# Weight sums loaded three rounds ahead in more buffers, and the sample attention stepped once in two places of a tile

## The chip, the cores and the metric

The kernel runs on one NeuronCore of a Trainium2 chip. The metric is the device time of one execution in microseconds (us). TensorE (PE) multiplies, VectorE (DVE), ScalarE (ACT) and GpSimd (POOL) do the elementwise work, and SyncE (SP) issues nearly all transfers. Each engine runs its own instructions strictly in order; what one engine needs of another, or of a transfer, is a semaphore wait ahead of the instruction.

## The reference

One layer of a hybrid decoder over a prompt of 2064 tokens (16 learned ones in front) and 8 samples of 4 tokens each:

```python
q, k, v, u = in_project(hp, norm_mix_pre[l], w_in[l])
att_o = swa_prompt(q, k, v, attn_sinks[l])           # sliding window of 128
ssm_o, hr, hi = ssm_mixer(u, ...)                     # complex diagonal scan, half-GLU
hp = hp + merge_out(att_o, ssm_o, ..., w_out[l], norm_mix_post[l])
hp = hp + sqrelu_mlp(hp, norm_mlp_pre[l], w_up[l], w_down[l], norm_mlp_post[l])
...                                                   # the same for the samples hs, with
att_o, nk, nv = swa_sample(q, k, v, cache_k_win[l], cache_v_win[l], pos_s, attn_sinks[l])

def sqrelu_mlp(h, g_pre, w_up, w_down, g_post):
    hn = rmsnorm(h, g_pre)
    a = jnp.square(jax.nn.relu(jnp.einsum('bsd,df->bsf', hn, w_up)))
    return rmsnorm(jnp.einsum('bsf,fd->bsd', a, w_down), g_post)
```

All data are float32, the model width is 1024, the MLP width 4096.

## The kernel before

Every large product is made of three TensorE matmuls (`mm3`, L111 to L113): each operand is split into a rounded high part (ACT, L96) and the rest (DVE, L97).

**The MLP** (`phase_mlp`) uses a seven-product scheme on 2 by 2 blocks of the weights (Strassen's, in Winograd's form). Some of its seven products need sums of weight blocks. These are made once, for each of 16 row blocks of `w_up` and of `w_down` and in two halves of 256 columns each, 64 pieces in all: `weight_sums` loads a piece of 128 x 4 x 256 (512 KB), four DVE subtractions of 128 x 256 (L1494 to L1497) turn it in place into the sums, and the result is stored to a scratch tensor in DRAM (`TU`, `TD`). `weight_sums` is a generator of three parts: load, subtractions, store. `sums_step` is one *round*: it moves every piece in flight by one part, then starts the next piece where a buffer is free. So before the change a piece is loaded in one round, subtracted in the next, stored in the one after.

Where the rounds are called: 30 pieces are subtracted on POOL during the attention (not touched by the change). 14 follow in `phase_mix`, three rounds (`SPT`) at the end of each of its tiles, with two buffers `wt` (`WTM`), on DVE. The last 20 are made in the first products of the MLP, one round in every fourth step from step 12 on, in five parts of the tile `Y`, which is free until then (`y_part`; at most three pieces in flight).

**The projection** (`phase_mix`) runs over 17 tiles of 128 tokens (`ORD`; the last holds the samples). In tile n: `proj_b` in two halves (the SSM part of the output projection, 12 matmuls each, tile `mm`), `turn` of tile n-2 (eight transposes, L1356), `proj_a` of tile n+2 (24 matmuls), `post_a` and `post_b` (norms and residual), loads, the three rounds. Ahead of tiles 0, 4, 8 and 12 stands the gate of the SSM part (`glu`). The attention of the samples is a generator `sample` of single steps; twice for each half of the cache it makes scores (L1265), the exponential (L1272), transposes of it (L1280, L1283) with a copy to SBUF on ACT (L1281, L1284), and the product with the values (L1288, L1289). Two of its steps are taken at the end of each tile, `advance(gen, 2)`.

**What sets the order.** In these two phases a scheduler with its own timing of the engines orders the instructions of each engine; `pace(x, after)` adds a constraint to it, without a wait on the chip, that x stands behind a given matmul. `LAST[0]` is the matmul written last. In the MLP a step is one block of weights times the kept operand: 12 matmuls. The weights `wr` come in seven buffers, and their split parts `wsh` and `wsl` are made three steps ahead of the matmuls (`ahead`).

Of the kernel before, what the change touches and what calls it, by code (L numbers as in the profile page):

```python
# [26 lines left out]
T2N = 25  # L27
MANUAL = {mybir.EngineType.PE, mybir.EngineType.DVE, mybir.EngineType.Activation, mybir.EngineType.Pool}
WTB = 2
WTM = 2  # L30
SLAST = 44
SPT = 3
WRB = 7
# [26 lines left out]
def hymba_step(ctx: ExitStack, tc: tile.TileContext, A, O):  # L60
# [648 lines left out]
    def y_part(n):  # L709
        return M["Y"].rearrange("p a c -> p (a c)")[:, 1024 * n:1024 * n + 1024].rearrange("p (q c) -> p q c", q=4)  # L710

    def sums_step(pl, eng, bufs, last=64, after=None):
        SUMS[:] = [x for x in SUMS if next(x, True) is None]
        if NSUM[0] < last and len(SUMS) < bufs:
            u, h = divmod(NSUM[0] % 32, 2)
            t = pl.tile([128, 4, 256], F32, name="wt", tag="wt", bufs=bufs) if pl else y_part(NSUM[0] % 5)
            x = weight_sums("ud"[NSUM[0] // 32], u, t, slice(256 * h, 256 * h + 256), eng, after)
            next(x)
            SUMS.append(x)
            NSUM[0] += 1  # L720
# [365 lines left out]
    def advance(gen, n=1):  # L1086
        for _ in range(n):
            next(gen, None)
# [141 lines left out]
    def phase_mix(outer, em, et):  # L1230
# [12 lines left out]
        def sample():  # L1243
# [3 lines left out]
            for hb in range(2):  # L1247
# [9 lines left out]
                yield  # L1257
                for kv in range(2):
                    st = gs.tile([128, 8], F32, name="sst", tag="sst", bufs=2)
                    e = gs.tile([128, 544], F32, name="se_", tag="se_", bufs=2)  # L1260
                    hv = slice(64 * kv, 64 * kv + 64)
                    for n in range(2):
                        c = slice(272 * n, 272 * n + 272)
# [110 lines left out]
        for n, i in enumerate(ORD):  # L1374
            if n % 4 == 0 and n < 12:
                for s in (n // 2 + 1, n // 2 + 2):
                    while s not in SO:
                        next(GLU)
            elif n == 12:
                while 7 not in SO:  # L1380
                    next(GLU)
            if n == 0:
                prep_b(ORD[1])
            proj_b(i, 0)
            if n > 1:
                turn(ORD[n - 2])
            proj_b(i, 1)
            if n + 2 <= NT:
                if ORD[n + 2] == NT:
                    advance(gen, 100)  # L1390
                proj_a(ORD[n + 2])
            post_a(i)
            advance(gen, 2)
            if n and n + 1 <= NT:
                prep_b(ORD[n + 1])
            post_b(i)
            if n + 2 <= NT:
                load_x(ORD[n + 2])
            if n + 4 <= NT:
                load_a(ORD[n + 4])  # L1400
            for _ in range(SPT):
                sums_step(gb, DVE, WTM, SLAST, LAST[0])
            if n == NT - 2:
                es.close()
                et.close()
                pre = pool(outer, "pre")
                mlp_open(pre)
                load_h(0)
                ahead(0)
        for k in range(4):  # L1410
            split_v(0, "u", 1, k)
        for x in SUMS:
            advance(x, 3)
        turn(ORD[NT - 1])
        turn(ORD[NT])
        return pre
# [69 lines left out]
        if p == ORDER[ph][1]:  # L1486
            DVE.tensor_tensor(x[2], x[0], x[2], op=OP.subtract)

    def weight_sums(ph, u, t, c=slice(0, 512), eng=DVE, after=None):
        x = SP.dma_start(t, WT[ph][0][u][:, :, c])  # L1490
        if after is not None:
            pace(x, after)
        yield
        eng.tensor_tensor(t[:, 0], t[:, 1], t[:, 0], op=OP.subtract)  # L1494
        eng.tensor_tensor(t[:, 1], t[:, 3], t[:, 1], op=OP.subtract)
        eng.tensor_tensor(t[:, 3], t[:, 3], t[:, 0], op=OP.subtract)
        eng.tensor_tensor(t[:, 2], t[:, 3], t[:, 2], op=OP.subtract)  # L1497
        yield
        SP.dma_start(WT[ph][1][u][:, :, c], t)
# [6 lines left out]
    def phase_mlp(pre):  # L1506
        with ExitStack() as es:
# [142 lines left out]
            for m, (b, ph, p, u, c) in enumerate(steps):  # L1650
                if (b, ph, p, u) == (0, "d", ORDER["d"][0], 0):
                    while NSUM[0] < 64 or SUMS:
                        sums_step(None, DVE, 3, 64, LAST[0])
                if ph == "d" and p == ORDER["d"][1] and u == 0 and b < 2:
                    load_h(b + 1)
                if m == 20:
                    pace(SP.dma_start(gpost, ap(A["g_mlp_post"], 0, [[0, 128], [1, D]])), LAST[0])
                if m + 2 < len(steps) and steps[m + 2][1] == "d":
                    split_v(*steps[m + 2])
                if m + 16 < len(steps) and steps[m + 16][1] == "u" and 8 <= u < 12:  # L1660
                    split_v(*steps[m + 16][:3], u - 8)
                if (b, ph) == (0, "u") and m >= 12 and m % 4 == 0:
                    sums_step(None, DVE, 3, 64, LAST[0])
                ahead(m)
                if last(b, ph, p):
                    if c == 0 and u % 3 == 1 and u < 9:
                        end_a(*(ENDS[0] + ENDS[1])[u // 3])
                    down_end(m, u, c)
                    continue
                (up if ph == "u" else down)(m, b, p, u)  # L1670
                if todo and u % 5 == 2:
                    todo.pop(0)()
                if ph == "d" and u == 15 and p in (5, 3):
                    todo += [lambda c=c, n=n, o=HN[b] * (p == 5), b=b: final(b, o + c, n)
                             for c, n in ((0, 128), (128, 128), (256, HN[b] - 256))]
# [115 lines left out]
```

## Time and profile before

| | |
|---|---|
| time, three runs | 2143.37, 2145.21, 2148.08 us; median 2145.21 |
| profiled execution | 2141.37 us |
| its span (first to last instruction) | 2139.6 us |
| granted TensorE clock, mean | 0.982 |
| attention and scan | to about 545 us of the span |
| projection | about 545 to 825 us |
| MLP | from about 825 us |

The stages overlap at their edges; the times are those of the span. TensorE is busy for 96% of the span. A busy time of an engine in a stretch of 10 us is read against the 10 us, and the clock beside it tells at which of its two levels (1.2 and 2.4 GHz) TensorE ran: 1.00 is the upper one throughout, 0.50 the lower one.

### The profile page before, as it was taken

Reading aid. Unit: us, or ns where it says so; the run is one execution under the profiler, and the core shown is the slowest. Engines: PE = TensorE matmul, PEld = TensorE weight load, DVE = VectorE, ACT = ScalarE, POOL = GpSimd, SP = SyncE. Lnnn points to the kernel's source line nnn. Section 1 sums busy time; section 2 is a strip of 40 time slices with the busy share of each in tenths; the row PEclk is TensorE's granted clock in tenths of the full one; section 3 lists DMA queues with packets and bytes.
Section 4 is the critical chain, followed back from the end, with each engine's and each line's share of the span. In section 5 each row is a group of like instructions: output and inputs, shape, how many; then the busy total and the mean of one; then the engine's idle time right before and its main releaser. Section 6 shows DMA issues by size and latency. Waiting matters only on the chain.

```text
span 2139.6 us, 35949 instructions
## 1 busy us (share of the span) xinstructions
PE 2055.6 (96%) x12524; PEld 1919.8 (90%) x12524; DVE 1573.4 (74%) x3269; ACT 1296.9 (61%) x2787; POOL 342.4 (16%) x371
## 2 busy tenths in 40 slices
PE   7899999988989899899999999999999999999998
PEld 7877888867778788889999999999999999999996
DVE  8946778776767466589866875878668758787686
ACT  6644666657646455368755554787555556875555
POOL 5502445343323341000000000000000000000001
PEclk9999999999999899999999999999999999999999
DMA  8896777766675356779554555555445554444554
GB/s 292 237 229 190 196 196 199 197 164 175 202 255 193 109 169 204 248 246 325 146 143 144 166 188 155 152 173 144 138 139 178 167 161 132 164 135 139 137 160 152
DMA packets 360670, 387.08 MB, mean 181 GB/s; under 512 B 105208, under 2 KB 250264, under 8 KB 360472
## 3 DMA queue, kind: packets, MB, share of 16 engines
q1 hardware_dynamic: 293800, 378.14, 57.9%
q10 hardware_dynamic: 65792, 4.20, 2.1%
q0 software_dynamic: 896, 2.46, 0.4%
q8 instruction: 98, 1.61, 0.3%
q14 instruction: 84, 0.69, 0.1%
HBM read 303.26 MB, written 82.46 MB: 180 GB/s over the span
## 4 chain that ended last, share of the span: by engine, by line
PE 80%; DMA 8%; DVE 6%; ACT 2%; issue 2%; POOL 1%; SPq 0%; POOLq 0%; DVEq 0%; ACTq 0%
PE mm L111 21%; PE mm L113 21%; PE mm L112 21%; PE mm L439 4%; DMA Y<-in_w_down_dram 3%; PE mm L867 2%; PE mm L440 2%; PE mm L815 1%; PE b L902 1%; PE mm L855 1%; DMA TD<-wt 1%; DMA wt<-in_w_down_dram 1%; PE b L940 1%; DMA qwr<-in_w_in_dram 1%; PE b L936 1%
## 5 line engine op out<-in xcount | busy, mean ns | idle before, releaser
L112 PE MATMUL mm<-vl,wsh 128*128 128x352 f32 (+1 forms) x2624 | 839.7, 320 | 0.0
L111 PE MATMUL mm<-vh,wsh 128*128 128x352 f32 (+1 forms) x2624 | 839.4, 321 | 0.0
L113 PE MATMUL mm<-vh,wsl 128*128 128x352 f32 (+1 forms) x2624 | 816.9, 321 | 11.7 <-DVE wsl L97 11.6
L96 ACT ACTIVATE wsh<-wr 128x512 fp32r<-128x512 f32 x684 | 430.3, 629 | 440.2 <-PE mm L112 426.0
L97 DVE TENSOR_TENSOR wsl<-wr,wsh 128x512 fp32r<-128x512 f32 x684 | 471.4, 690 | 182.2 <-ACT wsh L96 181.2
L113 PEld LDWEIGHTS mm<-vh,wsl 128*128 128x128 f32 x2624 | 489.1, 188 | 15.3 <-DVE wsl L97 15.0
L111 PEld LDWEIGHTS mm<-vh,wsh 128*128 128x128 f32 x2624 | 494.7, 189 | 0.2
L112 PEld LDWEIGHTS mm<-vl,wsh 128*128 128x128 f32 x2624 | 494.3, 188 | 0.0
L157 POOL TENSOR_TENSOR yst<-yst,nhalf 128x1 f32<-128x1 f32 (+2 forms) x15 | 12.4, 827 | 1252.1 <-DVE yst L156 1252.1
L1514 DVE TENSOR_TENSOR U<-U,mm 128x352 f32<-128x352 f32 (+3 forms) x240 | 140.0, 583 | 73.6 <-PE mm L113 73.0
L97 DVE TENSOR_TENSOR vl<-U,vh 128x352 fp32r<-128x352 f32 (+3 forms) x348 | 175.7, 506 | 1.4 <-ACT vh L96 1.0
L96 ACT ACTIVATE vh<-U 128x352 fp32r<-128x352 f32 (+3 forms) x348 | 162.9, 470 | 6.7 <-PE mm L112 6.4
L1547 ACT ACTIVATE U<-U 128x352 f32<-128x352 f32 (+1 forms) x192 | 93.0, 485 | 23.3 <-DVE U L1514 19.0
L1548 ACT ACTIVATE U<-U 128x352 f32<-128x352 f32 (+1 forms) x192 | 93.8, 490 | 4.4
L439 PE MATMUL mm<-qw,axh 128*128 128x512 f32 x224 | 85.9, 406 | 0.0
L111 PE MATMUL mm<-xh,uwh 128*128 128x264 f32 (+1 forms) x256 | 73.3, 297 | 12.9 <-DVE U L531 7.0
L112 PE MATMUL mm<-xl,uwh 128*128 128x264 f32 (+1 forms) x256 | 75.0, 296 | 0.0
L834 ACT ACTIVATE e<-e,mx 128x256 f32<-128x256 f32 x128 | 63.5, 497 | 16.8 <-DVE mx L828 16.7
L113 PE MATMUL mm<-xh,uwl 128*128 128x264 f32 (+1 forms) x256 | 72.8, 294 | 0.0
L857 ACT ACTIVATE PT<-mm 128x512 f32<-128x512 f32 x64 | 34.7, 593 | 57.3 <-PE mm L855 57.3
L111 PE MATMUL mm<-oh,psh 128*128 128x512 f32 (+1 forms) x136 | 58.8, 432 | 8.9 <-DVE pst L1210 6.4
L440 PE MATMUL mm<-qw,axh 128*128 128x256 f32 x224 | 63.2, 282 | 0.0
(367 smaller groups left out, 3508.9 us busy)
## 6 DMA issues: line engine op xcount, KB each, us to landing
wr<-TU SPq DMA_DIRECT2D x192, 256.0 KB
wr<-TD SPq DMA_DIRECT2D x192, 256.0 KB
wr<-in_w_down_dram SPq DMA_DIRECT2D x156, 256.0 KB
wr<-in_w_up_dram SPq DMA_DIRECT2D x144, 256.0 KB
wt<-in_w_up_dram SPq DMA_DIRECT2D x32, 512.0 KB
TU<-wt SPq DMA_DIRECT2D x32, 512.0 KB
Y<-in_w_down_dram SPq DMA_DIRECT2D x20, 512.0 KB
TD<-Y SPq DMA_DIRECT2D x20, 512.0 KB
```

What stands on the lines that cost most here:

```text
L96: ACT.activation(hi, src, AF.Copy)
L97: (eng or DVE).tensor_tensor(lo, src, r(hi), op=OP.subtract)
L111: PE.matmul(out, ah, bh, start=start, stop=False)
L112: PE.matmul(out, ah, bl, start=False, stop=False)
L113: LAST[0] = PE.matmul(out, al, bh, start=False, stop=stop)
L439: PE.matmul(pq[:n], lh(k), rh[k][:, 0:512], start=st, stop=sp_)
L440: PE.matmul(pkv[:n, :256], lh(k), rh[k][:, 512:768], start=st, stop=sp_)
L834: ACT.activation(e[:, j], e[:, j], AF.Exp, bias=mx[:, 1, j:j + 1], accum_out=mx[:, 3, j:j + 1])
L867: LAST[0] = PE.matmul(po[:, 256 * kv:256 * kv + 256], vr[:, sl[kb], kv, c0:c0 + 128], PT[u, kb][:, 256 * kv:256 * kv + 256], start=u == 0 ...
L1514: DVE.tensor_tensor(out, a, b, op=OP.add)
L1547: ACT.activation(x, x, AF.Relu)
L1548: ACT.activation(x, x, AF.Square)
```

## The change

Rounds: `weight_sums` has a parameter `wait`, the number of rounds from the load to the subtractions. It is 3 in the projection and in the MLP, and 1, as before, in the attention. The buffers `wt` grow from two to four and stand in the pool `gs` of the sample attention, which closes after tile 14; the tile `se_` of the sample attention has one buffer where it had two. In the MLP five pieces may be in flight, where it was three, in the same five parts of `Y`. The first subtraction of a piece is paced behind the matmul written last when its round comes.

Sample attention: one step of `sample` behind the first half of `proj_b` and one at the end of the tile, where there were two at the end.

```diff
-WTM = 2
+WTM = 4
-    def sums_step(pl, eng, bufs, last=64, after=None):
+    def sums_step(pl, eng, bufs, last=64, after=None, wait=1):
...
-            x = weight_sums("ud"[NSUM[0] // 32], u, t, slice(256 * h, 256 * h + 256), eng, after)
+            x = weight_sums("ud"[NSUM[0] // 32], u, t, slice(256 * h, 256 * h + 256), eng, after, wait)
...
-                    e = gs.tile([128, 544], F32, name="se_", tag="se_", bufs=2)
+                    e = gs.tile([128, 544], F32, name="se_", tag="se_", bufs=1)
...
             proj_b(i, 0)
+            advance(gen)
...
             post_a(i)
-            advance(gen, 2)
+            advance(gen)
...
             for _ in range(SPT):
-                sums_step(gb, DVE, WTM, SLAST, LAST[0])
+                if n < NT - 2:
+                    sums_step(gs, DVE, WTM, SLAST, LAST[0], 3)
...
-    def weight_sums(ph, u, t, c=slice(0, 512), eng=DVE, after=None):
+    def weight_sums(ph, u, t, c=slice(0, 512), eng=DVE, after=None, wait=1):
         x = SP.dma_start(t, WT[ph][0][u][:, :, c])
         if after is not None:
             pace(x, after)
-        yield
-        eng.tensor_tensor(t[:, 0], t[:, 1], t[:, 0], op=OP.subtract)
+        for _ in range(wait):
+            yield
+        x = eng.tensor_tensor(t[:, 0], t[:, 1], t[:, 0], op=OP.subtract)
+        if after is not None:
+            pace(x, LAST[0])
...
-                        sums_step(None, DVE, 3, 64, LAST[0])
+                        sums_step(None, DVE, 5, 64, LAST[0], 3)
...
-                    sums_step(None, DVE, 3, 64, LAST[0])
+                    sums_step(None, DVE, 5, 64, LAST[0], 3)
```

Three places where the order of an engine moves. First SP in the MLP's first product: `Y` rows are the loads of pieces, `TD` rows their stores, `wr` rows the weights, one row for each step of the MLP. Before:

```order
L1490 DMA Y<-in_w_down_dram 128x4x256
L1446 DMA wr<-TU 128x512 x4
L1490 DMA Y<-in_w_down_dram 128x4x256
L1499 DMA TD<-Y 512x1x256
L1446 DMA wr<-TU 128x512 x3
L1499 DMA TD<-Y 512x1x256
L1446 DMA wr<-TU 128x512
```

and now:

```order
L1496 DMA Y<-in_w_down_dram 128x4x256
L1452 DMA wr<-TU 128x512 x4
L1496 DMA Y<-in_w_down_dram 128x4x256
L1452 DMA wr<-TU 128x512 x2
L1508 DMA TD<-Y 512x1x256
L1452 DMA wr<-TU 128x512 x2
L1496 DMA Y<-in_w_down_dram 128x4x256
L1452 DMA wr<-TU 128x512 x2
L1508 DMA TD<-Y 512x1x256
```

Before, a store stands three rows of `wr` behind the load of the same piece. Now it stands 14 behind it: the stores seen are those of pieces loaded three and four loads earlier, and the load that follows a store goes into the part of `Y` that this store empties.

Second DVE in the projection, around the end of tile 3 (`wt` rows are subtractions, L1333, L1341 and L1342 the norms and residual, L1210 a norm's factor). Before:

```order
L97 TENSOR_TENSOR pal<-pat,pah 128x512
L1494 TENSOR_TENSOR wt<-wt 128x256
L1495 TENSOR_TENSOR wt<-wt 128x256
L156 TENSOR_SCALAR pst<-pst 128x1
L1496 TENSOR_TENSOR wt<-wt 128x256
L1210 TENSOR_SCALAR pst<-mm 128x1
L1494 TENSOR_TENSOR wt<-wt 128x256
L1497 TENSOR_TENSOR wt<-wt 128x256
```

and now:

```order
L1333 SCALAR_TENSOR_TENSOR po<-mm,pst,po 128x512
L1501 TENSOR_TENSOR wt<-wt 128x256
L1339 TENSOR_TENSOR pst<-pst 128x1
L1504 TENSOR_TENSOR wt<-wt 128x256
L156 TENSOR_SCALAR pst<-pst 128x1
L1505 TENSOR_TENSOR wt<-wt 128x256
L1501 TENSOR_TENSOR wt<-wt 128x256
L1210 TENSOR_SCALAR pst<-mm 128x1
L1506 TENSOR_TENSOR wt<-wt 128x256
L1341 SCALAR_TENSOR_TENSOR po<-po,pst,gpost 128x1024
```

The twelve subtractions of a tile stand among its own rows as before, but those of three pieces that were loaded a tile earlier.

Third PE in a late tile of the projection, at the third product of the sample attention (L1280 and L1283 the transposes, L1288 and L1289 the product, L1356 a `turn`). Before:

```order
L113 MATMUL mm<-oh_5363,pal 128x512
L1280 MATMUL mm<-ident,se__7401 128x128 x4
L1283 MATMUL mm<-ident,se__7401 32x128
L1356 MATMUL b_7758<-ident,po 128x128 x8
L1288 MATMUL mm<-cv,spT 128x64 x4
L111 MATMUL mm<-oh_5816,psh 128x512
```

and now, the transposes:

```order
L1209 MATMUL mm<-ones,pq_7424 128x2
L1356 MATMUL b_7632<-ident,po 128x128 x8
L1280 MATMUL mm<-ident,se__7324 128x128 x4
L1283 MATMUL mm<-ident,se__7324 32x128
L111 MATMUL mm<-oh_5816,psh 128x512
```

and the product, 36 matmuls of the projection further down:

```order
L112 MATMUL mm<-ol_5364,pah 128x512
L113 MATMUL mm<-oh_5363,pal 128x512
L1288 MATMUL mm<-cv,spT 128x64 x4
L1289 MATMUL mm<-vns,spT 128x64
L111 MATMUL mm<-oh_5816,psh 128x512
```

Only a `turn` stood between the transposes and the product that needs their copy, here and at the fourth product; now half of `proj_b` and the whole of `proj_a` stand there. At the first and second product it is the other way round: 48 matmuls stood between, now 12, with a `turn` at the first.

## Rows read from the trace of the kernel before

**Rows 1.** The page, part 1, TensorE: busy us (share of span), instructions.

```profile
PE 2055.6 (96%) x12524; PEld 1919.8 (90%) x12524; DVE 1573.4 (74%) x3269; ACT 1296.9 (61%) x2787; POOL 342.4 (16%) x371
```

**Rows 2.** Stretches: length, then busy us of each engine, clock, DMA share, GB/s.

```profile
620.00:630.00 10.00, 3.64 (x17) 2.87 (x17) 7.16 (x15) 4.45 (x9) 2.12 (x3) 0.74 0.74 231
880.00:890.00 10.00, 8.01 (x52) 7.66 (x50) 5.26 (x12) 3.68 (x8) 0.00 (x0) 1.00 0.70 218
1000.00:1010.00 10.00, 10.00 (x67) 10.00 (x66) 9.24 (x19) 9.81 (x23) 0.00 (x0) 1.00 1.07 395
```

**Rows 3.** PE's waits at 560-700, 700-760, 840-965 us: total, times, longest.

```profile
PE mm L111 <- DVE pst L1210: 9.0, 2, 6.4
...
PE mm L1288 <- ACT spT L1281: 5.5, 2, 2.9
...
PE mm L113 <- DVE wsl L97: 11.6, 10, 2.1
```

**Rows 4.** Stretches cut where the clock was at its lower level, columns as above.

```profile
604.35:607.76 3.41, 3.41 (x17) 3.38 (x16) 1.31 (x3) 2.40 (x5) 0.98 (x1) 0.50 1.00 356
624.83:631.66 6.83, 4.03 (x10) 3.16 (x11) 6.78 (x14) 4.63 (x11) 1.66 (x2) 0.50 0.83 258
706.75:713.58 6.83, 6.65 (x19) 5.17 (x19) 0.00 (x0) 1.42 (x3) 0.55 (x1) 0.50 0.63 192
740.88:747.71 6.83, 6.48 (x19) 5.18 (x19) 0.62 (x2) 1.47 (x3) 0.00 (x0) 0.50 0.50 154
908.14:911.55 3.41, 3.41 (x14) 3.41 (x14) 2.13 (x5) 0.63 (x1) 0.00 (x0) 0.50 0.94 274
925.20:928.61 3.41, 3.41 (x14) 3.41 (x13) 3.41 (x9) 1.73 (x4) 0.00 (x0) 0.50 0.59 136
```

**Rows 5.** Waits of all engines and of SP's queue, 560-1000 us.

```profile
DVE Y L1494 <- DMA Y<-in_w_down_dram: 40.7, 13, 5.4
DVE wt L1494 <- DMA wt<-in_w_down_dram: 16.7, 9, 2.8
...
SPq L1490 <- DMA TD<-wt: 27.2, 10, 3.8
```

**Rows 6.** The chain in order of time, 480-1020 us: start, us, transfer.

```profile
574.03 6.21 DMA wt<-in_w_down_dram
...
597.24 3.73 DMA TD<-wt
...
872.63 5.10 DMA TD<-Y
...
897.51 7.12 DMA Y<-in_w_down_dram
...
910.54 4.88 DMA wr<-TU
```

**Rows 7.** DVE in order of time, 623-628 us; idle time before in brackets.

```profile
624.07 0.42 DVE L1494 TENSOR_TENSOR wt<-wt 128x256 f32<-128x256 f32 x1 [2.05 <-DMA wt<-in_w_down_dram]
```

**Rows 8.** PE and ACT in order of time, 690-752 us.

```profile
697.46 0.39 PE L113 MATMUL mm<-oh,pal 128*128 128x512 f32 x1
...
697.69 0.39 PE L111 MATMUL mm<-oh,pah 128*128 128x512 f32 x1
...
703.32 1.04 PE L1356 MATMUL b<-ident,po 128*128 128x128 f32 x8
...
706.77 0.25 ACT L1284 ACTIVATE spT<-mm 32x128 f32<-32x128 f32 x1
```

**Rows 9.** DVE in order of time, 940-1000 us, one step of the fourth product.

```profile
941.55 0.68 DVE L97 TENSOR_TENSOR wsl<-wr,wsh 128x512 fp32r<-128x512 f32 x1
942.15 0.41 DVE L1496 TENSOR_TENSOR Y<-Y 128x256 f32<-128x256 f32 x1
...
943.32 0.68 DVE L97 TENSOR_TENSOR wsl<-wr,wsh 128x512 fp32r<-128x512 f32 x1
```

**Rows 10.** Line L1211, 560-820 us: ns of one, least, median, most; first and last.

```profile
L1211 POOL TENSOR_TENSOR pst<-pst,nhalf x30: 541/552/1534, 565.1 to 810.7; 128x1 f32<-128x1 f32 x28, 32x1 f32<-32x1 f32 x2
```

More of the change, by code (lines that the diff above doesn't have):

```diff
@@ L1401, in phase_mix @@
             for _ in range(SPT):
-                sums_step(gb, DVE, WTM, SLAST, LAST[0])
+                if n < NT - 2:
+                    sums_step(gs, DVE, WTM, SLAST, LAST[0], 3)
             if n == NT - 2:
+                for x in SUMS:
+                    advance(x, 6)
+                SUMS.clear()
                 es.close()
@@ L1412, in phase_mix @@
         for x in SUMS:
-            advance(x, 3)
+            advance(x, 6)
+        SUMS.clear()
         turn(ORD[NT - 1])
```

## The prediction

> **What bounds the kernel now.** I read the page first: TensorE is busy 96% of the span [rows 1], so only time in which TensorE stands still, or runs at the lower clock, can be won. The table by stretches of 10 us shows where that is [rows 2]: a full stretch of the MLP holds 67 matmuls, and in the stretches the change touches there are 17 (620 to 630 us) and 52 (880 to 890). TensorE's own waits then name three places [rows 3]. **Place A**, the projection around its fifth tile: 9.0 us in two waits, for a DVE factor (L1210) that frees a bank. **Place B**, 700 to 750 us: 5.5 us in two waits of the sample attention's product (L1288) for the ACT copy of its transposes. **Place C**, the first 120 us of the MLP: 11.6 us in ten waits for `wsl`, the low part of the weights, from DVE. DVE is late at A and C for one reason: it stands before the first subtraction of a piece until the piece has landed, 16.7 us over nine times in the projection and 40.7 us over 13 in the MLP [rows 5]. One such wait, 2.05 us until 624.07 us, stands in [rows 7]; the longer of TensorE's two waits for L1210 ends a little over 3 us later, with six other instructions of DVE between.
>
> Each of these places also lowers the clock. Six stretches at 0.50 follow or lie in the waits [rows 4]; what TensorE does in them takes twice its time, so half of the busy time in each is lost: 1.7 and 2.0 us at A, 3.3 and 3.2 at B, 1.7 and 1.7 at C.
>
> So the three places cost A 9.0 + 3.7 = 12.7, B 5.5 + 6.5 = 12.0, C 11.6 + 3.4 = 15.0 us, together 39.7 us. That is the most that the change can win by the mechanism that I see. From about 1000 us on TensorE is full [rows 2], and nothing there is edited.
>
> **The subtractions in the MLP (C).** A step of the MLP is 12 matmuls, 10 us / 67 x 12 = 1.79 us [rows 2]. By the orders of SP and DVE, a piece is loaded two to three steps ahead of its first subtraction before, 13 steps ahead now (a row of `wr` on SP leaves when the split of seven steps earlier frees one of the seven buffers; so a load's place among the `wr` rows tells its place among the splits on DVE). That is 3.6 to 5.4 us against a transfer of up to 7.1 us [rows 6], and now 23 us. The wait of DVE has to go, even if SP holds the load back by several us. What is late next? DVE itself, in the fourth product: one step of it takes DVE 943.32 - 941.55 = 1.77 us with one subtraction in it [rows 9], as good as TensorE's 1.79. The change takes no subtraction away and puts none closer together there; but what else falls to DVE in that product finds no room. I leave one piece's four subtractions, 4 x 0.41 = 1.6 us [rows 9], as lost: C wins 13.4 of 15.0.
>
> The new wait: a load now goes into the part of `Y` whose store was issued one to six rows of `wr` earlier, 14 to 17 before. SP stands until that store has landed, and the weights queue behind it. Such a store takes 5.1 us [rows 6]; SP waited for such stores already in the projection, 27.2 us over ten times [rows 5]. A row of `wr` may leave seven steps, 12.5 us, before its split is due and takes 4.9 us [rows 6], so 7.6 us are spare, and the wait is covered. If the cover is gone, see the slow rival.
>
> **The subtractions in the projection (A).** A piece is now subtracted one tile after its load. But a load must wait until the store of the piece four loads back, whose buffer it takes, has landed: subtraction, store, load and the next subtraction in that buffer go round in about one tile. That takes about 2 us for the subtractions, 3.7 to 5.1 us for the store and 6.2 us for the load [rows 6], 12 to 13 us, plus what SP lets it queue. A tile has 48 matmuls of 0.23 us [rows 8], a `turn` of 1.0 us [rows 8] and some small ones: a little over 12 us. So the first pieces of tiles 2 to 4 will arrive about when they are needed, where before they were sure to be late. I take a DVE wait of 4 us instead of 16.7; by the old ratio (9.0 of TensorE for 16.7 of DVE) and with its share of the clock that leaves 2.5 us or so: A wins 10.2 of 12.7. The bounds: nothing left (12.7), or half of it left (6.4). Nothing is removed from any queue: 14 loads, 56 subtractions and 14 stores remain. The transfers of `pat`, `px`, `H1D` and `HTD` stand behind the waiting loads on SP, as they did before.
>
> **The sample attention (B).** At the two waits the copy ends 3.7 us after the transposes (707.02; the `turn` behind them begins at 703.32), and only that `turn` lies between [rows 8]. Now 36 matmuls of 0.23 us, 8.3 us, lie between. Both waits go, and with them the two stretches at the lower clock, which begin at 706.75 and 740.88, at the end of these idle times. At the first and second product the cover falls from 48 matmuls to 12, 2.8 us (3.8 with the `turn` at the first), against the same 3.7 us for the copy: up to 0.9 us lost at the second. I take 1 us for both. One buffer for `se_` costs nothing: the next scores come after the transposes that read it, in both orders. B wins 11 of 12.0.
>
> **The sum.** 13.4 + 10.2 + 11 = 34.6 us. The profiled execution took 2141.4 us, so its like would take 2106.8. The runs shown have a median 3.8 us above it, 2145.2, and the time will be judged against that: 2145.2 - 34.6 = 2110.6.
>
> **The rivals.** *The projection keeps its waits.* The round of store and load takes longer than a tile, and DVE waits for pieces as before, only a tile later. For it speaks that SP already waits 27.2 us for stores there; against it that four buffers give each piece a tile. It gives 13.4 + 11 = 24.4 us, 2121. Chance 0.13.
>
> *The norms on POOL stretch.* L1211 takes 0.55 us mostly, once 1.53 [rows 10], and ACT's `po` waits for it. Should denser runs of subtractions make it 1 us longer at two norms of each of five tiles, and none of it be covered, 10 us go back: 2121. It comes out like the first rival; chance 0.05. The Trainium skill, "SBUF — State Buffer", section "Who interferes with whom", says that a DVE instruction with two SBUF inputs contends with a GpSimd instruction that reads SBUF; the subtractions are of that kind, and the spread of rows 10 is in line with it, though the median says that it is rare.
>
> *Weights come late in the MLP.* SP's wait for stores moves into the queue of the weights, and what DVE gains at C TensorE loses waiting for `wr`. If it just eats the gain of C: 10.2 + 11 = 21.2 us, 2124. Chance 0.06. *The slow side* is the same place, if it costs more than it ever cost before. It decides where wait and transfer together pass the 12.5 us of cover: a store of 7 us, as long as the slowest load [rows 6], then `wr` slowed to the same 7, is 14 us, 1.5 us over. With 15 loads that reuse a part of `Y`, 15 x 1.5 = 23 us, and as much again for the lower clock after each, 46 us, against the 21.2 won elsewhere: 2170. Against it: with TensorE full and the last pieces in flight the transfers ran at 395 GB/s [rows 2] without a late weight. Chance 0.05.
>
> *The change does not do what it says:* the scheduler could have set the subtractions right behind their loads again. The orders speak against it, 13 steps instead of two or three, so 0.02: 2145 less B's 11, 2134.
>
> **How the numbers follow.** The forecast has 0.69, the rivals above 0.13, 0.05, 0.06, 0.05 and 0.02. The forecast's own range is 2101 (all 39.7 won, and 4 us for the runs' spread) to 2117 (A half won, some loss at C). To leave out no more than 2 in 10 the range takes in the two rivals at 2121 and the one at 2124: 2101 to 2126. A difference under 0.2%, 4.3 us, can't be told from no change here. All cases but the slow one are faster by more than that; I keep 0.03 for mixtures that end near zero. Faster 0.92, same 0.03, slower 0.05.
>
> **What would show it.** Right: DVE's wait for `Y` gone from 40 us to a few, TensorE's waits for `wsl` before 960 us under 2 us, no wait of L1288 over 1 us, no stretch at 0.50 between 700 and 1000 us, the MLP starting about 21 us earlier; SP's waits for stores in the MLP new, several us each, with no engine waiting behind them. Wrong: DVE still idle before L1501 in tiles 2 to 4 (first rival), ACT's `wsh` waiting for `wr` (the weights), POOL's L1211 often over 1 us.

## The result

The changed kernel took 2107.78 us (median of four runs, 2107.61 to 2109.57) against 2145.77 us before: a ratio of 0.9823, 95% interval 0.9806 to 0.9840. Its profiled execution took 2107.68 us, with a span of 2105.9. The forecast was 2110.6 us, within 2101 to 2126.

First the page of the changed kernel, part 1, busy time by engine, as in [rows 1]:

```profile
PE 2040.7 (97%) x12524; PEld 1910.5 (91%) x12524; DVE 1576.1 (75%) x3269; ACT 1294.4 (61%) x2787; POOL 345.1 (16%) x371
```

The instructions are as many as before; TensorE's busy time is 14.9 us shorter, at a mean clock of 0.988 instead of 0.982. Its stretches, columns as in [rows 2]:

```profile
590.00:600.00 10.00, 8.93 (x46) 7.36 (x45) 8.70 (x20) 4.74 (x12) 3.69 (x6) 0.86 1.07 372
...
620.00:630.00 10.00, 10.00 (x58) 8.60 (x58) 6.95 (x11) 5.79 (x13) 2.14 (x3) 1.00 0.49 157
...
880.00:890.00 10.00, 10.00 (x68) 10.00 (x67) 8.67 (x19) 5.11 (x10) 0.00 (x0) 1.00 0.93 298
...
960.00:970.00 10.00, 8.44 (x55) 8.16 (x54) 5.79 (x14) 5.73 (x14) 0.00 (x0) 1.00 1.06 395
```

At 620 to 630 us there are 58 matmuls instead of 17, at 880 to 890 us 68 instead of 52. Two stretches fall short: one at 0.86, and one with 55 matmuls. TensorE's waits, 560 to 830 and 830 to 1000 us (total, times, longest), name the cause of each:

```profile
PE mm L1288 <- ACT spT L1281: 1.1, 1, 1.1
...
PE mm L111 <- ACT wsh L96: 1.6, 1, 1.6
```

Of [rows 3] nothing over 1 us is left but a wait for `spT`, and that one stands at the sample's first product (595.8 us), where none stood before. The second line is new: `wsh` is the high part of the weights, from ACT. The waits of DVE, 560 to 1000 us, and of SP's queue, 560 to 800 and 800 to 1000 us:

```profile
DVE wt L1501 <- DMA wt<-in_w_down_dram: 0.8, 2, 0.6
...
SPq L1496 <- DMA TD<-wt: 1.4, 2, 0.9
...
SPq L1496 <- DMA TD<-Y: 18.0, 5, 4.7
```

DVE's 40.7 and 16.7 us for pieces [rows 5] are gone but for 0.8. SP's wait for stores of `wt` was 27.2 us [rows 5]; its wait for stores of `Y` is new.

**Where the 33.7 us are.** The start of TensorE's instructions cuts each span at the same places. The projection begins, for this table, at the first norm of `proj_b` (L1209, its third pair of matmuls in the trace; the two pairs before it belong to `proj_a` of the first two tiles), the MLP at its first matmul with `vh`. Before:

```profile
546.94 0.28 PE L1209 MATMUL mm<-ones,pq 128*128 128x2 f32 x2
...
812.93 0.32 PE L111 MATMUL mm<-vh,wsh 128*128 128x336 f32 x1
```

and after:

```profile
551.91 0.28 PE L1209 MATMUL mm<-ones,pq 128*128 128x2 f32 x2
...
796.37 0.32 PE L111 MATMUL mm<-vh,wsh 128*128 128x336 f32 x1
```

So the stages ahead of the projection became 5.0 us longer, the projection 21.5 shorter (266.0 to 244.5), the MLP 17.2 shorter (1326.7 to 1309.5). Each kernel below is cut in the same way (us; the variants are described further down). A is 546.9 to 636.0 us of the profile before, B is 674.2 to 754.3, and the same matmuls of L1209 bound them in the other kernels:

| kernel | begins | A | B | projection | MLP |
|---|---|---|---|---|---|
| before | 546.9 | 89.1 | 80.1 | 266.0 | 1326.7 |
| before, again | 550.8 | 88.7 | 79.8 | 265.3 | 1330.4 |
| after | 551.9 | 79.0 | 67.2 | 244.5 | 1309.5 |
| after, again | 551.7 | 78.5 | 67.0 | 244.4 | 1310.0 |
| MLP rounds alone | 552.5 | 88.6 | 79.8 | 265.2 | 1310.2 |
| projection rounds alone | 553.0 | 76.2 | 76.5 | 249.8 | 1327.6 |
| sample split alone | 550.8 | 91.4 | 66.8 | 256.0 | 1326.4 |
| first tile unsplit | 551.9 | 75.6 | 67.0 | 242.0 | 1311.5 |
| subtractions held | 551.1 | 90.8 | 80.2 | 267.8 | 1308.4 |
| subtractions not held | 555.4 | 76.9 | 66.5 | 242.7 | 1329.4 |
| activations later | 551.1 | 79.6 | 67.0 | 244.9 | 1308.5 |
| both of these edits | 555.2 | 77.1 | 67.1 | 243.0 | 1308.3 |
| one round behind | 552.2 | 76.0 | 66.5 | 241.4 | 1308.5 |
| one round behind, again | 547.9 | 76.1 | 66.5 | 241.5 | 1308.4 |

Of the three kernels profiled twice (one round behind is one order of instructions in both rows) a stage repeats within 1 us, except the MLP before (1326.7 and 1330.4) and the beginning. That lies between 547 and 555 us whatever the kernel.

### The profile page after: what moved, and what is told of

It reads as the page before. It is cut to its first block, busy times and chain, and to the rows that moved or that the text cites. A ratio compares the mean times of both kernels' runs of the same rounds, so it can differ in the third digit from the quotient of the medians.

```text
span 2105.9 us, 35968 instructions
## 1 busy us (share of the span) xinstructions
PE 2040.7 (97%) x12524; PEld 1910.5 (91%) x12524; DVE 1576.1 (75%) x3269; ACT 1294.4 (61%) x2787; POOL 345.1 (16%) x371
## 4 chain that ended last, share of the span: by engine, by line
PE 86%; DVE 6%; DMA 3%; ACT 2%; issue 2%; POOL 0%; SPq 0%; ACTq 0%; POOLq 0%; DVEq 0%
PE mm L111 23%; PE mm L112 23%; PE mm L113 23%; PE mm L439 4%; PE mm L867 2%; PE mm L440 2%; PE mm L815 2%; PE b L902 1%; PE mm L855 1%; DMA qwr<-in_w_in_dram 1%; PE b L940 1%; DVE U L1523 1%; PE b L1597 1%; PE b L936 1%; PE b L1356 1%
## 5 line engine op out<-in xcount | busy, mean ns | idle before, releaser
L111 PEld LDWEIGHTS mm<-xh,uwh 128*128 128x128 f32 x256 | 49.9, 199 | 13.5 <-DVE U L531 7.5
## 6 DMA issues: line engine op xcount, KB each, us to landing
wr<-TU SPq DMA_DIRECT2D x192, 256.0 KB
wr<-TD SPq DMA_DIRECT2D x192, 256.0 KB
wr<-in_w_down_dram SPq DMA_DIRECT2D x156, 256.0 KB
wr<-in_w_up_dram SPq DMA_DIRECT2D x144, 256.0 KB
```

The source lines that it names most:

```text
L111: PE.matmul(out, ah, bh, start=start, stop=False)
```

## The parts by themselves

**The MLP's rounds alone:** the kernel before, with

```diff
-sums_step(None, DVE, 3, 64, LAST[0])
+sums_step(None, DVE, 5, 64, LAST[0], 3)
```

at both places of the MLP, and there the *tie* of the subtractions: the two lines of the change that pace a piece's first subtraction behind the matmul written last.

> The kernel before with the change of the MLP's rounds alone (five Y parts, subtractions three rounds after the load); projection and sample as before. Theory (the three places are independent, each part of the change is worth what its own stretch gained): the first matmul of the MLP stays at 813 us within 1 us, no PE wait for wsl between 813 and 960 us, and the matmuls after that come 15 to 16.5 us earlier, so about 2130 us against 2145.8. Rival (the MLP's gain in the changed kernel came in part from what the projection left behind: its rounds in flight and the wr loads that it had ahead): wsl waits remain in the first 60 us of the MLP, gain under 10 us, 2136 us or more.

2128.87 us, ratio 0.9906 (0.9885 to 0.9928). The projection is that of before (265.2 us) and the MLP that of after, 1310.2 us, with no wait for `wsl`. The parts of the change are independent here. The first matmul of the MLP came at 817.8 us, not at the expected 813, because this profile's projection began 5.6 us later.

**The projection's rounds alone:** the kernel before, with the tie, `se_` in one buffer, and

```diff
-WTM = 2
+WTM = 4
...
-                sums_step(gb, DVE, WTM, SLAST, LAST[0])
+                if n < NT - 2:
+                    sums_step(gs, DVE, WTM, SLAST, LAST[0], 3)
```

> The kernel before with the projection's rounds alone (four buffers, subtractions three rounds after the load); the sample attention keeps both its steps after a tile's first part of the output, the MLP's rounds are as before. Theory: the stretch around the fifth tile loses its 12 to 14.5 us, the wait for spT at 700 to 750 us (12.0 us with its half-clock stretch) and the MLP's wsl waits (15 us) remain, and the projection begins within 1 us of before: about 2132 us. Rival (part of that 14.5 us belongs to the split, which took the first sample product out of the same stretch): 5 us or less gained there, the first product's wait for spT or a wait for pst at 600 to 640 us still in the trace, 2139 us or more.

2137.84 us (five runs, 2132.19 to 2139.40, the quickest one profiled), 0.9942 (0.9921 to 0.9963); the expected 2132 us is met by two of the five. Against the mean of the two profiles of before A falls by 12.7 us, all of its 12.7. B falls too, by 3.5, though both waits for `spT` stand in it. TensorE's waits for `spT`, 560 to 850 us:

```profile
PE mm L1288 <- ACT spT L1281: 6.1, 2, 3.2
```

and the stretches behind the first and with the second of them, columns as in [rows 2]:

```profile
702.40:705.80 3.40, 3.40 (x9) 2.62 (x9) 0.00 (x0) 0.47 (x1) 0.00 (x0) 0.50 0.98 292
...
730.00:740.00 10.00, 7.11 (x42) 5.77 (x40) 2.97 (x8) 4.48 (x8) 2.40 (x5) 1.00 0.49 159
```

The first wait is followed by 3.4 us at the lower clock; at the second the clock is 1.00 throughout. Before, each of the two stood beside 6.83 us at 0.50 [rows 4], the second with the same wait of 2.89 us.

**The sample split alone:** the kernel before, with

```diff
             proj_b(i, 0)
+            advance(gen)
...
-            advance(gen, 2)
+            advance(gen)
```

> The kernel before with the sample attention's two steps per tile taken apart (one after the first half of the output projection, one after the second) and nothing else. Theory (the later entry into the projection in the changed kernel is the split's doing, since it puts the sample's copies of the caches and its loads ahead of two loads of the gate on SP's queue): the first normalised half of the first tile ends 4 to 6 us later than before, the wait for spT at 700 to 750 us goes (12 us), a wait for spT of 1 us with a half-clock stretch comes near 596 us (2.8 us), waits at the fifth tile and in the MLP stay: 4 to 6 us faster in all, about 2141 us. Rival (the late entry comes from the rounds' first loads, which the changed kernel issues in another order): entry within 1 us of before, 9 to 12 us faster, about 2135 us.

2139.39 us, 0.9957 (0.9944 to 0.9970). Against the mean of before B becomes 13 us shorter, A 2.5 longer (a wait for `spT` of 2.0 us at 596.4), the projection as a whole 9.7 shorter. On top of the projection's rounds the split is worth less: 249.8 to 244.4, 5.4 us. The beginning at 550.8 us looked like the theory's, but the MLP's rounds alone, with the old order of the sample's copies, begin at 552.5.

**The first tile unsplit, and before once more.** To settle the beginning, the changed kernel with

```diff
             proj_b(i, 0)
-            advance(gen)
+            if n:
+                advance(gen)
...
-            advance(gen)
+            advance(gen, 1 if n else 2)
```

> The changed kernel, but in the projection's first tile both sample steps come after the tile, as before the change, so that the gate's last loads of zu and one of pat stand ahead of the sample's cache copies on SP's queue again. Theory (those copies held up the gate and the first tile by 5 us): the first normalised half of the first tile is back at 547 us within 1 us, all later work 4 to 6 us earlier, about 2103 us against 2107.8. Rival (the loads are not late, the gate's delay is of the order of its own instructions on ACT and DVE): entry still at 551 to 552 us and the total within 1.5 us of the changed kernel's.

2107.05 us, 0.9804 (0.9782 to 0.9825), beginning at 551.9 us, the same as with the split. The rival was right on the beginning. Behind it the projection is 2.5 us shorter (242.0), with a wait of 0.2 us left for the sample's first product.

> The kernel before once more, to see how far its early stages shift between executions. The four variants so far all began the projection (first normalised half) at 550.8 to 553.0 us, two of them with the old order of the sample's copies, against 546.9 us in the first profile of before. Theory now (the 5 us at the entry belong to the executions, not to the change): this profile too begins the projection at 549 to 553 us, with projection (266 us to the first MLP matmul) and MLP (1326.7 us) as in the first profile within 2 us each. Rival (546.9 us is what the old program does and each of the variants disturbs it): 546 to 548 us again.

One run, 2148.29 us, beginning at 550.8 us; its MLP, 1330.4 us, missed the expectation by 3.7. So the 5.0 us are not seen to be the change's: the first profile of before was of its quickest execution, 2141.37 us of all from there to 2155.9 on the chips used. One part of the change does reach the stages ahead of the projection. The subtractions on POOL during the attention are made by the same function and are tied too; in the kernel with nothing but the tie (further down) the order on POOL, SP, ACT and DVE differs from before between 444 and 552 us. The beginning doesn't show it: 547.9 to 555.2 us in the eight profiles with that tie, 546.9 to 555.4 in the six without. What makes the projection begin anywhere from 547 to 555 us was not studied.

## Distance, buffers, or the tie

**One round behind.** The changed kernel with the old distance of one round, all buffers and the tie kept:

```diff
-                    sums_step(gs, DVE, WTM, SLAST, LAST[0], 3)
+                    sums_step(gs, DVE, WTM, SLAST, LAST[0], 1)
...
-                    sums_step(None, DVE, 5, 64, LAST[0], 3)
+                    sums_step(None, DVE, 5, 64, LAST[0], 1)
```

> The changed kernel with its four and five buffers, but each round's subtractions one round behind its load, as before the change, in the projection and in the MLP. Theory (the gain is the distance between load and subtraction; more buffers only make room for it): the MLP's wsl waits come back in full (15 us), DVE waits for wt in the projection again, one long wait for pst of PE near 600 to 640 us (6 to 13 us) with its half-clock stretch; the sample's gain of 12 us at 700 to 750 us stays: 2130 to 2136 us. Rival (the loads were held back by the stores of their buffers, so that more buffers are enough in the projection): no DVE wait for wt over 2 us there, only the MLP's 15 us come back, about 2123 us; by the second rival (buffers do all of it) 2108 us.

2104.90 us, 0.9796 (0.9778 to 0.9813). My theory fell: nothing came back, in the projection (241.4 us) or in the MLP (1308.5), so a distance of three rounds is not what the gain needs. How far a subtraction stands behind its load was read from starts, SP's issue and DVE's first subtraction of that piece. Before:

```profile
897.51 0.89 SPq L1490 DMA_DIRECT2D Y<-in_w_down_dram  x1
...
904.65 0.42 DVE L1494 TENSOR_TENSOR Y<-Y 128x256 f32<-128x256 f32 x1 [4.82 <-DMA Y<-in_w_down_dram]
```

7.1 us, of which DVE stood 4.82. After:

```profile
884.10 1.50 SPq L1496 DMA_DIRECT2D Y<-in_w_down_dram  x1
...
907.79 0.42 DVE L1501 TENSOR_TENSOR Y<-Y 128x256 f32<-128x256 f32 x1
```

23.7 us and no wait. The median of the twenty pieces is 6.3 us before (waits included), 23.4 after, 8.8 one round behind, and 8.8 is enough. In steps, counted as in the prediction from the orders of SP and DVE, the first ten pieces stand two to three steps behind their loads before, 12 to 13 after, and five one round behind. What the old distance in the code lacked was the tie, two lines that the prediction passed over. Two kernels test it by itself.

**Subtractions held:** the kernel before and nothing but the tie:

```diff
-        eng.tensor_tensor(t[:, 0], t[:, 1], t[:, 0], op=OP.subtract)
+        x = eng.tensor_tensor(t[:, 0], t[:, 1], t[:, 0], op=OP.subtract)
+        if after is not None:
+            pace(x, LAST[0])
```

> The kernel before, with one thing of the change: a round's subtractions are tied to the matmul at their own place in the order, so that the scheduler can't put them earlier. Buffers (two and three), one round from load to subtraction and the sample's steps are as before. With the tie each subtraction of the MLP stands 8 weight splits behind the one that was last when its Y part was asked for, without it 5. Theory (the tie alone makes the MLP's gain; a distance of 8.7 us against transfers of 5 to 7 is enough): no PE wait for wsl after 820 us, MLP 1310 us from its first matmul to the end instead of 1326.7 to 1330; in the projection two buffers still make a load wait for the store of its buffer, so the wait for pst at the fifth tile (12.7 us) and that for spT (12 us) stay: 2129 to 2133 us. Rival (the tie is enough there too): the stretch at the fifth tile loses 12 us as well, 2117 to 2121 us. Second rival (the tie does little, five Y parts in use make the gain): wsl waits of over 8 us in the MLP, 2140 us or more.

2126.14 us (the profiled execution 2129.14), 0.9891 (0.9870 to 0.9911), 3 us below the expected 2129 to 2133. The MLP has its whole gain, 1308.4 us, with these rows for a piece:

```profile
899.28 0.55 SPq L1490 DMA_DIRECT2D Y<-in_w_down_dram  x1
...
908.01 0.42 DVE L1494 TENSOR_TENSOR Y<-Y 128x256 f32<-128x256 f32 x1
```

The projection has gained nothing. DVE's and SP's waits there, 560 to 1000 and 560 to 820 us:

```profile
DVE wt L1494 <- DMA wt<-in_w_down_dram: 18.1, 11, 2.6
...
SPq L1490 <- DMA TD<-wt: 28.6, 10, 4.4
```

With two buffers SP holds ten loads until a store of a piece has landed, as before [rows 5]. The tie was not overruled there; it had nothing to change: from 552 to 838 us the order of the instructions is that of before on every engine.

**Subtractions not held:** the changed kernel without it.

```diff
-        x = eng.tensor_tensor(t[:, 0], t[:, 1], t[:, 0], op=OP.subtract)
-        if after is not None:
-            pace(x, LAST[0])
+        eng.tensor_tensor(t[:, 0], t[:, 1], t[:, 0], op=OP.subtract)
```

> The changed kernel without the tie of a round's subtractions to the matmul at their place; the distance of three rounds, the four and five buffers and the split sample are kept. VectorE's order in the MLP is then the old one, instruction by instruction, since the scheduler takes the subtractions forward to where it believes their loads landed. Theory (the tie is what puts the distance into effect): the MLP's 15 us of wsl waits are back; in the projection four buffers keep the loads from waiting for stores, so at most half of the fifth tile's 12.7 us is back: 2122 to 2130 us. Rival (three rounds of distance and the buffers do it without the tie): within 2 us of the changed kernel, 2107 to 2110 us.

2129.14 us, 0.9903 (0.9883 to 0.9922). DVE's waits 560 to 1000 us, TensorE's 830 to 1000, SP's 560 to 800:

```profile
DVE Y L1501 <- DMA Y<-in_w_down_dram: 44.1, 16, 5.2
...
DVE wt L1501 <- DMA wt<-in_w_down_dram: 0.9, 1, 0.9
...
PE mm L113 <- DVE wsl L97: 14.1, 11, 2.3
...
SPq L1496 <- DMA TD<-wt: 2.7, 2, 2.2
```

All of the MLP's loss is back, with a distance of three rounds in the code: the scheduler took the subtractions forward, and the median piece is again subtracted 6.3 us after its load. From 764 to 986 us the order on every engine is that of the kernel before, so three rounds and five parts of `Y` by themselves changed nothing there. The projection keeps its gain (242.7 us): there four buffers free SP of the stores (2.7 us of waiting instead of 27.2), and pieces land in time.

So the two places were cured by different things: the MLP by the tie alone, whatever the rounds and buffers; the projection by four buffers. Four buffers without tie and without distance were not run, so that each of those is needless there follows only from leaving out one at a time; nor were two buffers with the distance of three rounds.

## The late weight, and a faster version

In the changed kernel five weights stood behind the second half of the activations (`H`) that the second block needs. SP in order of time:

```profile
954.95 0.39 SPq L1512 DMA_DIRECT2D H<-HTD  x1
955.43 0.57 SPq L1508 DMA_DIRECT2D TD<-Y  x1
956.09 4.13 SPq L1452 DMA_DIRECT2D wr<-in_w_up_dram  x5
```

`load_h` was tied to its own step:

```diff
-            SP.dma_start(M["H"][:, 4 * c:4 * c + 4, :2 * HN[b]], HTD[512 * c:512 * c + 512, COL0[b]:COL0[b] + 2 * HN[b]]
+            x = SP.dma_start(M["H"][:, 4 * c:4 * c + 4, :2 * HN[b]], HTD[512 * c:512 * c + 512, COL0[b]:COL0[b] + 2 * HN[b]]
                          .rearrange("(k p) t -> p k t", p=128))
+            if b:
+                pace(x, LAST[0])
```

> The changed kernel, with the load of the second block's activations (H, two halves of 1408 KB) tied to its own step in the order of the MLP, behind the rounds, instead of going out at 934 and 955 us, among them. Theory (the one late weight of the changed kernel, 1.56 us of PE at 967 us, comes from five wr loads that stand right behind the second half of H, 4.2 us late): no PE wait for wsh between 940 and 1000 us, 1.6 us faster, about 2106 us; if the two halves are late instead where they now stand, a wait for wsh of up to 3 us shows between 990 and 1040 us and the time is 2107 to 2109 us. Rival (the weights are late because SP waits for the stores of Y parts ahead of them): the wait at 967 us stays at 1 us or more.

2109.52 us, 0.9815 (0.9796 to 0.9834). No wait of TensorE is left between 830 and 1060 us and the MLP is 1.0 to 1.5 us shorter. The weight was late because of that 1408 KB transfer, not because SP waits for stores, for these waits are the same as after (18.0 us). SP's queue, 800 to 1000 us:

```profile
SPq L1496 <- DMA TD<-Y: 18.1, 5, 4.6
```

A late weight stands in other kernels with three rounds and the tie in the MLP too, 2.4 us with the MLP's rounds alone and 1.9 with the first tile unsplit, there with 3.4 us at the lower clock behind it and an MLP of 1311.5 us. In the whole time a gain of this size can't be seen. With the first tile unsplit as well:

> Both edits on top of the changed kernel: the sample's two steps of the first tile behind that tile, and the load of H behind the rounds. The first alone shortened the stretch from the first normalised half to the first MLP matmul from 244.5 to 242.0 us (no wait for spT at 596 us and no half-clock stretch behind it), the second is expected to take 1.6 to 1.9 us from the MLP. Theory (both hold and add): about 2104 us, 3 to 4.5 us under the changed kernel. Rival (they shift the same transfers onto one another): 2106.5 us or more.

2107.77 us, 0.9805 (0.9784 to 0.9827): inconclusive as a time. By stretches both edits hold (projection 243.0, MLP 1308.3, some 3 us together), but this profile began 3.3 us later than that of after.

The version with one round of distance does both without either edit: no spell at the lower clock near 600 us in its two profiles (a wait of 1.5 us for `spT` stands in one of them), no late weight. It was run again beside the changed kernel on one chip, with at most three pieces in flight in the MLP; the order of its transfers and of every engine from 22 us on is that of the first one:

> The changed kernel once more, beside the next run on one chip. 2106 to 2110 us; the first normalised half at 551 to 555 us, the wait for spT at 596 us and the one for wsh at 967 us as in its first profile.

> The changed kernel with one round from load to subtraction, as before the change, subtractions tied, four buffers in the projection, three live rounds allowed in the MLP instead of five: instruction by instruction on every engine the kernel that took 2104.9 us. Theory (a shorter distance costs nothing as long as it covers the transfer, and its other order on SP spares the weight that came late at 967 us and the sample's wait at 596 us, 1.6 and 2.8 us): 2 to 4 us under the changed kernel on the same chip, about 2104.5 us. Rival (the 3 us between them were the chip's): the two within 1.5 us.

2109.89 us (2107.88 to 2111.15), 0.9813 (0.9793 to 0.9833), and 2103.83 us (2099.59 to 2108.11), 0.9789 (0.9767 to 0.9811). The intervals overlap and one run of each lies in the other's spread, but the stretches agree over two profiles of each: 2.9 to 3.1 us less in the projection, 1.0 to 1.6 in the MLP, about 4.3 in all. The other 2 us between the medians would have to lie ahead of the projection, which began 3.8 us earlier in this profile.

## The prediction, step by step

**The mechanism and the three places** were right: the long waits in [rows 3] are gone, and DVE's waits for pieces went as said. Of the signs named, two came out otherwise: a wait of L1288 over 1 us is left (1.1 and 2.2 us in the two profiles of after), and the MLP starts 16.5 us earlier in the profile, not 21, since the projection began 5.0 us later. The forecast sum of 34.6 us stands against 33.7 in the profiles and 38.0 in the medians of the runs, and that it comes so near is in part luck: the three places won 21.5 + 17.2 = 38.7 us, near the bound of 39.7, and the later beginning took back 5.0. On the chip of the later runs the ratio was 0.9813 and the medians lay 40.3 us apart (2150.16 and 2109.89).

**C was too small,** 13.4 us against 17.2, which is above the bound of 15.0 too. The reserve of 1.6 us for a full DVE was not needed. The bound counted only the listed idle time and the clock. TensorE before, at the longest wait but one of the ten:

```profile
885.63 0.31 PE L111 MATMUL mm<-vh,wsh 128*128 128x336 f32 x1
885.78 0.32 PE L112 MATMUL mm<-vl,wsh 128*128 128x336 f32 x1
888.08 0.42 PE L113 MATMUL mm<-vh,wsl 128*128 128x336 f32 x1 [1.99 <-DVE wsl L97]
888.34 0.32 PE L111 MATMUL mm<-vh,wsh 128*128 128x336 f32 x1
```

Undisturbed, these matmuls start 0.15 us apart and overlap, though each is listed with 0.32. Here 885.78 to 888.34 is 2.56 us for two steps of 0.15, so the stop cost 2.26 us where 1.99 is listed. Counted so, the ten stops cost 14.3 us where 11.6 are listed. At the lower clock the bound was a little too high: 12 matmuls start in each of the two stretches [rows 4], 0.28 us apart, which is 1.5 us lost and not 1.7. Together 14.3 + 3.0 = 17.3 us, against 17.2 won. In the second profile of before the ten stops cost 17.8 us (15.1 listed), with two such stretches 20.8; its MLP is 20.4 to 20.9 us longer than that of after.

**Why C went** was right in kind, since a load that is far enough ahead of its subtraction ends DVE's wait, and incomplete in what makes it so. The prediction read the 13 steps, 23 us, correctly from the orders, but did not ask how much of them is needed or which line of the change makes them. Five steps, 8.8 us, do, and the tie makes them; rounds and buffers without it leave two to three. The rival that the scheduler sets the subtractions back behind their loads, which I gave 0.02, is what happens in the MLP without the tie: 1329.4 us, some 20 more than with it.

**A** was sized at 10.2, with 4 us of DVE's waits left (which by the prediction's own ratio cost 4 x 12.7 / 16.7 = 3.0 us, not 2.5). Its rounds alone won 12.7, with 2.1 us of such waits left there and 0.8 in the changed kernel: the round of store and load is not tight. The reason given, that a piece is subtracted a tile after its load, is not what it takes, for with one round A is as short (76.0 us). In its place the runs show the four buffers: SP's waits for stores of `wt` fell from 27.2 us [rows 5] to 1.4.

**B** was sized at 11. The split won 9.7 us alone and 5.4 on top of the rounds, for two causes. The first product cost 2.5 us in A, not 1. The prediction took its cover, 3.8 us, against the 3.7 us that the copy needs at the third product. At the first the copy ends 5.0 us behind the end of its transposes, and 4.6 us behind them already before (585.85 to 590.48), so the price stood in the trace at another row. In the changed kernel (PE and ACT):

```profile
590.68 0.27 PE L1283 MATMUL mm<-ident,se__6352 128*32 128x128 f32 x1
...
595.67 0.25 ACT L1284 ACTIVATE spT<-mm 32x128 f32<-32x128 f32 x1
595.84 1.10 PE L1288 MATMUL mm<-cv,spT 128*128 128x64 f32 x8 [1.07 <-ACT spT L1281]
```

A wait of 1.1 to 2.2 us follows from it, and in the changed kernel this stretch at the lower clock:

```profile
597.30:600.72 3.42, 3.42 (x9) 2.72 (x9) 1.92 (x4) 2.88 (x6) 1.80 (x3) 0.50 1.09 376
```

And I put the two half-clock stretches of 6.83 us, 6.5 us of loss, down to B's own waits; with the projection's rounds in place 3.5 us of that were gone with the waits still there. Why is not shown. Against the mean of the two profiles of before the rounds won 15.9 and the split then 5.4; I had forecast 10.2 and 11, which is the same sum.

**The new waits.** SP's 18.0 us for stores held up nothing, as said. Weights came late once, 1.6 us, from a transfer that I had not looked at. The norms on POOL stretched little; L1211 in the changed kernel, 560 to 800 us, as in [rows 10]:

```profile
L1211 POOL TENSOR_TENSOR pst<-pst,nhalf x31: 537/552/1531, 564.3 to 794.1; 128x1 f32<-128x1 f32 x29, 32x1 f32<-32x1 f32 x2
```

Median and maximum are those of before, but they hide what the prediction read as one slow norm: 11 of the 30 before took over 0.7 us and five of these about 1.5, now 14 of 31 and again five. Before, on DVE and POOL:

```profile
675.56 1.37 DVE L1342 TENSOR_TENSOR px<-px,po 128x1024 f32<-128x1024 f32 x1
...
675.81 1.53 POOL L1211 TENSOR_TENSOR pst<-pst,nhalf 128x1 f32<-128x1 f32 x1
```

In the two profiles of before and the two of after a norm or residual of 128 x 1024 (L1341, L1342; two inputs from SBUF) is already running on DVE 21 times when L1211 begins, and each of these takes 1.46 to 1.53 us, ending about 0.4 us behind it; six times L1211 begins first and takes 0.55 to 0.73 us. So the traces agree with the contention that the Trainium skill describes ("SBUF — State Buffer", section "Who interferes with whom") between a DVE instruction with two SBUF inputs and a GpSimd instruction that reads SBUF. The subtractions' other places brought no more of it, though: L1211 took 23.5 us in all before (30 of them) and 24.6 now (31), against 24.3 (31) in the second profile of before.

## What to carry to other kernels

Where a scheduler orders the instructions, its order sets how far a consumer stands behind its load, not the number of rounds in the code (6.3 us with three rounds, 8.8 with one round and the tie): tie the consumer to its place first, measure the distance in the trace against the transfer, and add buffers only where a queue waits for their release. Test each ingredient alone, since the two places here looked alike and needed different ones. And profile the kernel before more than once: the projection began 4 us apart in two profiles of one kernel and 8 us apart over all fourteen, more than some of the terms in the sum.

## What the runs showed of the hardware that I had not expected

The lower clock does not follow from the length of a wait alone. Before, a wait of 2.89 us for `spT` stood beside 6.83 us at 0.50 (from 740.88). With the projection's rounds alone a wait of the same 2.89 us left the clock at 1.00. Both came 33 to 34 us after another wait (2.57 and 3.22 us) with a stretch at 0.50 behind it (6.83 and 3.4 us), so that earlier wait does not tell them apart; what does is not shown.

A stop of TensorE costs more than the idle time listed for it, some 0.27 us at each of the ten stops in the MLP before. The rows above show why: matmuls that start 0.15 us apart are listed with 0.32 us, so the end of the one before the stop covers part of it, and the first one behind it starts 0.26 us ahead of the next.

A small GpSimd instruction (L1211, 128 x 1) of 0.55 us took 1.46 to 1.53 us, 21 times of 21, where a VectorE instruction of 128 x 1024 with two inputs from SBUF had begun before it, and at most 0.73 where it began first.
